# Emptying the bank of attention values: one ScalarE copy of all 128 partitions, a transfer between partitions, and GpSimd's add, in place of a ScalarE copy of 64 and VectorE's add

## The chip, the cores and the metric

The kernel runs on one core of a Trainium2 chip. A core has TensorE (PE; its weight loads are a row of their own, PEld), VectorE (DVE), ScalarE (ACT), GpSimd (POOL) and SyncE (SP), which issues the kernel's transfers. The metric is the device time of one execution, in microseconds. The kernel before took 1499.21 us, the median of three runs (1498.03 to 1502.22).

## What is computed

One layer of a streaming encoder, for one sequence of 1024 positions, 1024 channels, all in float32. Two attention branches of 8 heads of 64 channels run on one projection of the input; branch a is softmax attention over a band of the last 9 chunks of 64 positions with a learned bias by distance, branch b is stick-breaking attention:

```python
h = x @ w_in                                  # q, k, v of a; q, k, v of b; two gates
# a: softmax(q k^T / 8 + bias[distance]) @ v  over the own chunk and the 8 before it
# b: z = q k^T / 8;  w = sigmoid(z) * prod over keys between of (1 - sigmoid(z));  w @ v
y_a = chunk_band_attention(qa, ka, va, rel_bias) @ w_proj_a
y_b = stick_breaking_attention(qb, kb, vb) @ w_proj_b
mix = (sigmoid(ga + b_gate_a) * y_a + sigmoid(gb + b_gate_b) * y_b) @ w_out
x = layer_norm(alpha * x + mix, ln1_g, ln1_b)
g, u = split(x @ w_ffn_in)
x = layer_norm(alpha * x + (silu(g) * u) @ w_ffn_out, ln2_g, ln2_b)
```

## The kernel before

Matmul operands are float32 values split in two: `hi`, the value rounded to a shorter format that PE multiplies fast, and `lo`, the rest. `split` (L107) makes them: ScalarE copies `hi` (L108), VectorE subtracts for `lo` (L109). A product is then three matmuls, or two where one operand is kept as the pair.

The stages in time are: the input projection, 0 to about 355 us; the attention with what is laid between it, 355 to 687 us; branch b's output projection, the merge and the first norm; the feed-forward part, which ends the run. The change is in the attention.

There the work is in 8 pairs of heads (`i` 0 to 3 branch a, 4 to 7 branch b), two heads (`h` 0 and 1) to a pair and two groups of 512 queries (`g` 0 and 1) to a head. For each block of 128 queries a head makes a tile of attention weights (`soft_block`, L483, and `stick_block`, L513): scores on PE (L461, L462), then for a the sum with the bias and its minimum on VectorE (L492), the exponential on ScalarE (L497), the reciprocal on VectorE (L499) and the scaling on GpSimd (L500); for b two sigmoids on ScalarE (L525, L526), two running products on VectorE (L529, L533; their second input is a tile in PSUM) and the multiplication on GpSimd (L535). The value steps (`value_steps`, L537) then go through the key blocks, 8 of them for g = 0 and 4 for g = 1: `turn` transposes weights on PE (L556) into a PSUM bank `tp` and splits it to `pt`; `mult` multiplies with the values (L569, L570) into the bank `pv`.

The values of a head are kept as 128 columns, 64 of `hi` and 64 of `lo`, so that one matmul does both: the bank `pv` holds the products with `hi` in partitions 0 to 63 and those with `lo` in partitions 64 to 127. At the last key block of a group the bank is emptied: ScalarE copies the lower half to the head's 64 partitions of the pair's tile `yt` (L575), VectorE adds the upper half from PSUM (L576). There is one such bank (`BANKS`, `pv=1`). When all four quarters of a pair are in, SyncE stores the tile in `y_dr` (L578); for the pair i = 7 it stays in SBUF. `reload_y` (L624) brings the others back for the output projections.

Between the steps fill work is laid, for which a generator hands out single matmuls: the gate products (`gate`, L411; L418) and then branch a's output projection (L603; gated on VectorE, L606), 18 matmuls for each head of a and 42 for each of b (`FILL`). Weights for them, yraw and gA tiles are loaded by SyncE and split by ScalarE and GpSimd (L402, L630). The value step that is multiplied lags its transposes by two (`LAG`), and the weight blocks are made a given number ahead (`LEAD`).

The order on each engine isn't that of the source lines: a planner places the instructions engine by engine from the source order, the dependences and its own idea of costs, and every engine then runs its list in order. The tiles of a tag share the given number of buffers (`SLOTS`, here `yt=3`); one whose buffer is still read waits for it. All transfers are issued by SyncE, in its list's order; one that waits holds up those behind it.

Of the kernel before, what the change touches and what calls it, by code (L numbers as in the profile page):

```python
# [14 lines left out]
ALU = mybir.AluOpType  # L15
# [3 lines left out]
P = 128  # L19
# [3 lines left out]
DH = 64  # L23
# [23 lines left out]
def hybrid_trunk_kernel(ctx: ExitStack, tc, x, xt, w_in, b_gate, rel_bias, w_proj,  # L47
# [6 lines left out]
    nc = tc.nc  # L54
# [7 lines left out]
    def slot(tag, name, dtype=F32):  # L62
        return pool.tile([P, 1024], dtype, tag=tag, name=name, bufs=SLOTS[tag])
# [10 lines left out]
    def bank(tag, name):  # L74
        return ps.tile([P, HW], F32, tag=tag, name=name, bufs=BANKS[tag])

    def dram(name, n):
        return [dr.tile([P, 1024], F32, name=f"{name}{i}") for i in range(n)]
# [3 lines left out]
    dma = nc.sync.dma_start  # L82
# [12 lines left out]
    y_dr = dram("y_dr", 8)  # L95
# [11 lines left out]
    def split(dst_h, dst_l, src):  # L107
        nc.scalar.copy(dst_h, src)  # L108
        nc.vector.tensor_tensor(dst_l, src, dst_h.bitcast(F32), ALU.subtract)  # L109
# [325 lines left out]
    def load_qk(hd):  # L435

        i, h = hd["i"], hd["h"]
        n = 2 * i + h
        q, k = (d[i][h * P:(h + 1) * P] for d in (q_dr, k_dr))
        for key, part in (("qs", None), ("kh", 0), ("kl", DH)):  # L440
            t = hd[key] = slot(key, f"{key}{n}", F32R)
            if part is None:
                dma(t.bitcast(F32), q)
            else:
                for half in (slice(0, DH), slice(DH, P)):
                    dma(t[half].bitcast(F32), k[part:part + DH])
        if hd["br"] == 0:
            hd["bias"] = rel_bias_tile(hd["n"])

    def load_v(hd):  # L450

        n = 2 * hd["i"] + hd["h"]
        t = slot("v", f"v{n}", F32R)
        dma(t.bitcast(F32), v_dr[n])
        hd["v"] = t.rearrange("p (t c) -> p t c", t=8)
# [57 lines left out]
    def stick_block(hd, b, be):  # L513
# [7 lines left out]
        for c0, n in cuts:  # L521
# [12 lines left out]
                                             kp[:, s0 - 1:s0], ALU.mult, ALU.bypass)  # L534
            nc.gpsimd.tensor_tensor(be[:, m0:e], be[:, m0:e], kp[:, m0 - 1:e - 1], ALU.mult)  # L535

    def value_steps(hd, g, wt):  # L537

        br, h = hd["br"], hd["h"]
        reach = (4, 8)[br]  # L540
        q0 = 4 * g
        nm = f"{'ab'[br]}{hd['n']}_{g}"
        pv = []

        kbs = [4, 5, 6, 7, 3, 2, 1, 0] if g == 0 else [7, 6, 5, 4]
        steps = []
        for i, kb in enumerate(kbs):
            lo_q = max(q0, kb - reach)
            hi_q = min(q0 + 3, kb)
            n = (hi_q - lo_q + 1) * P  # L550
            pts = []

            def turn(kb=kb, lo_q=lo_q, hi_q=hi_q, n=n, pts=pts):
                tp = bank("tr", f"tp_{nm}_{kb}")
                for qb in range(lo_q, hi_q + 1):
                    tr(tp[:, (qb - lo_q) * P:(qb - lo_q + 1) * P],  # L556
                       wt[qb - q0][:, (kb - qb) * P:(kb - qb + 1) * P], ident)
                pt = slot("pt", f"pt_{nm}_{kb}", F32R)
                split(pt[:, 0:n], pt[:, HW:HW + n], tp[:, 0:n])
                pts.append(pt)  # L560

            def mult(i=i, kb=kb, lo_q=lo_q, n=n, pts=pts):
                v = hd["v"]
                if i == 0:
                    pv.append(bank("pv", f"pv_{nm}"))
                last = i == len(kbs) - 1
                cs = slice((lo_q - q0) * P, (lo_q - q0) * P + n)
                pt = pts[0]
                mm(pv[0][:, cs], v[:, kb, :], pt[:, 0:n], start=(i == 0), stop=False)  # L569
                mm(pv[0][:, cs], v[:, kb, :], pt[:, HW:HW + n], start=False, stop=last)  # L570
                if last:
                    yt = hd["yt"]()
                    r = slice(h * DH, (h + 1) * DH)
                    gs = slice(g * HW, (g + 1) * HW)
                    nc.scalar.copy(yt[r, gs], pv[0][DH:P])  # L575
                    nc.vector.tensor_tensor(yt[r, gs], pv[0][0:DH], yt[r, gs], ALU.add)  # L576
                    if h == 1 and g == 1 and hd["i"] < 7:
                        dma(y_dr[hd["i"]], yt)  # L578

            steps.append((turn, mult))  # L580
        return steps

# [57 lines left out]
    def fill_until(t):  # L640
        while state["t"] < t and not state["done"]:
            try:
                state["t"] += next(fill)
            except StopIteration:
                state["done"] = True
# [35 lines left out]
    for si, (hd, g, st, box) in enumerate(vsteps):  # L681
        hidx, pos = si // nhead, si % nhead
        if hidx < 15 and pos == 1:
            load_qk(heads[hidx + 1])
        if hidx < 15 and pos == 4:
            load_v(heads[hidx + 1])
        while wi < min(hidx * 8 + LEAD[pos], len(wunits)):
            wunits[wi]()
            wi += 1
        if st == 0:  # L690
            steps_of[(hidx, g)] = value_steps(hd, g, box)
        turn, mult = steps_of[(hidx, g)][st]
        turn()
        last = goal
        goal += FILL[hd["br"]] / nhead
        fill_until(0.5 * (last + goal))
        pend.append(mult)
        if len(pend) > LAG:
            pend.pop(0)()
        fill_until(goal)  # L700
# [361 lines left out]
```

## Time and profile before

| | us |
|---|---|
| median of three runs | 1499.21 |
| lowest, highest | 1498.03, 1502.22 |
| the profiled execution, its own time | 1501.38 |
| its span in the profile | 1499.3 |
| attention with its fill work | 355 to 687 |

In the page's rows and in answers on the trace, times are in us from the start of the span. A row of a group reads: line, engine, operation, output <- inputs, shapes, count | busy time, mean in ns | idle time of the engine just before it and who ended it. A row of a wait reads: who waited, on which line, <- for whom, total us, how often, the longest. A row of the timeline reads: start, length, instruction, and in brackets the idle time before it.

### The profile page before, as it was taken

To read this page: it belongs to the slowest core of one execution; us is meant where nothing else is said; L and a number is where in the kernel's file an instruction comes from. 1 tells how busy PE (TensorE), PEld (TensorE's weight loads), DVE (VectorE), ACT (ScalarE), POOL (GpSimd) and SP (SyncE) were. 2 spreads that over 40 slices of the span, in tenths; PEclk is the share of its full clock that TensorE was granted. 3 is DMA by queue.
4 is the path that set the end of the run, shared out by engine and by line. 5 is a ranking of instruction groups with operands and counts; after the bars stand their busy time and mean duration, and the time that the engine had idled before them with its cause. 6 is when DMAs were issued, how large, how long until landed. Compare 5 with 4: busy or idle time off the path is not lost. (4 is left out here: it accounts for less than half of the span.)

```text
span 1499.3 us, 19075 instructions
## 1 busy us (share of the span) xinstructions
PE 1440.3 (96%) x6728; PEld 1179.6 (79%) x6728; DVE 1043.9 (70%) x1702; ACT 679.7 (45%) x1174; POOL 282.4 (19%) x322
## 2 busy tenths in 40 slices
PE   8999999999999999899999899999999998999997
PEld 6788888887887777777787688888888886778886
DVE  8865556435878887887849966767777755767757
ACT  6444444336877778775303534444444433111201
POOL 0000000004344558650014000000000003341016
PEclk9999999999999999999999999999999999999999
DMA  6555555247754556647502123444444456677602
GB/s 211 163 175 169 168 168 170 98 144 213 206 170 142 159 165 204 187 157 280 183 0 87 62 100 121 152 155 155 155 155 154 155 189 232 245 249 267 234 8 105
DMA packets 81215, 244.05 MB, mean 163 GB/s; under 512 B 10064, under 2 KB 10064, under 8 KB 81120
## 3 DMA queue, kind: packets, MB, share of 16 engines
q1 hardware_dynamic: 81120, 242.84, 48.5%
q8 instruction: 53, 0.87, 0.2%
q14 instruction: 42, 0.34, 0.1%
HBM read 162.03 MB, written 80.77 MB: 162 GB/s over the span
## 5 line engine op out<-in xcount | busy, mean ns | idle before, releaser
L535 POOL TENSOR_TENSOR w_b<-w_b,kp_b 128x511 f32<-128x511 f32 (+3 forms) x96 | 97.5, 1021 | 51.5 <-DVE kp_b L533 40.6
L950 POOL TENSOR_TENSOR tda<-wdR,wdL 128x512 f32<-128x512 f32 x8 | 10.7, 1340 | 491.6 <-DMA wdR<-in_w_ffn_out_dram 477.8
L533 DVE TENSOR_TENSOR_SCAN kp_b<-kp_b,ident_ps 128x384 f32<-128x384 f32 (+6 forms) x88 | 78.3, 890 | 4.1
L479 POOL MEMSET bias<- 64x64 f32 x8 | 1.2, 146 | 334.5 <-ACT bias L478 334.5
L745 POOL TENSOR_TENSOR mv<-mv,neghalf 128x1 f32<-128x1 f32 x16 | 23.9, 1495 | 211.4 <-DVE mv L744 211.4
L525 ACT ACTIVATE kp_b<-sc_b 128x512 f32<-128x512 f32 (+3 forms) x96 | 48.5, 505 | 31.4 <-PE sc_b L462 26.5
L183 DVE TENSOR_TENSOR c<-sxp,c 128x512 f32<-128x512 f32 x16 | 11.1, 692 | 73.9 <-issue 40.7
L925 DVE TENSOR_TENSOR x<-dx,x 128x512 f32<-128x512 f32 x64 | 43.6, 689 | 24.6 <-PE dx L995 24.6
L109 DVE TENSOR_TENSOR pt_b<-tp_b,pt_b 128x512 fp32r<-128x512 f32 (+1 forms) x96 | 51.1, 543 | 10.9 <-ACT pt_b L108 10.4
L170 PE MATMUL szf<-x1S63h,wcf 128*128 128x512 f32 x176 | 57.8, 389 | 0.0
L500 POOL TENSOR_SCALAR w_a<-w_a,st_a 128x640 f32<-128x640 f32 (+2 forms) x64 | 42.6, 671 | 67.2 <-DVE st_a L499 49.6
L556 PE MATMUL tp_b<-ident,w_b 128*128 128x128 f32 x288 | 49.3, 277 | 5.2 <-DVE pt_b L109 2.8
L108 ACT CAST pt_b<-tp_b 128x512 fp32r<-128x512 f32 (+1 forms) x96 | 47.1, 497 | 13.7 <-PE tp_b L556 13.2
L109 DVE TENSOR_TENSOR sl<-h,sl 128x512 fp32r<-128x512 f32 x56 | 38.4, 686 | 20.2 <-ACT sl L108 20.2
L108 ACT CAST sl<-h 128x512 fp32r<-128x512 f32 x56 | 34.8, 621 | 35.6 <-PE syf L170 17.1
L109 DVE TENSOR_TENSOR pt_a<-tp_a,pt_a 128x512 fp32r<-128x512 f32 (+1 forms) x96 | 45.5, 484 | 7.6 <-ACT pt_a L108 7.3
L497 ACT ACTIVATE w_a<-w_a,st_a 128x640 f32<-128x640 f32 (+2 forms) x64 | 44.6, 698 | 12.8 <-DVE st_a L492 11.2
L118 PE MATMUL ops<-wh_o,ml 128*128 128x512 f32 x128 | 50.2, 392 | 0.2 <-DVE ml L109 0.2
L115 PE MATMUL ops<-wh_o,mh 128*128 128x512 f32 x128 | 50.2, 392 | 0.0
L116 PE MATMUL ops<-wl_o,mh 128*128 128x512 f32 x128 | 49.9, 390 | 0.0
L556 PE MATMUL tp_a<-ident,w_a 128*128 128x128 f32 x240 | 44.8, 277 | 5.0 <-POOL w_a L500 2.4
L833 ACT ACTIVATE h<-sxf 128x512 f32<-128x512 f32 x22 | 13.2, 598 | 79.6 <-PE sxf L170 79.6
(1881 smaller groups left out, 4833.4 us busy)
## 6 DMA issues: line engine op xcount, KB each, us to landing
s_dr<-sl SPq DMA_DIRECT2D x112, 256.0 KB, 2.2
sd<-s_dr SPq DMA_DIRECT2D x56, 512.0 KB, 5.2
wLf<-in_w_ffn_in_dram SPq DMA_DIRECT2D x22, 512.0 KB, 4.4
wRf<-in_w_ffn_in_dram SPq DMA_DIRECT2D x22, 512.0 KB, 3.6
wLp<-in_w_in_dram SPq DMA_DIRECT2D x17, 512.0 KB, 5.3
wRp<-in_w_in_dram SPq DMA_DIRECT2D x17, 512.0 KB, 4.0
v_dr<-v SPq DMA_DIRECT2D x16, 512.0 KB, 4.3
qs<-q_dr SPq DMA_DIRECT2D x16, 512.0 KB, 6.2
```

The source lines that it names most:

```text
L108: nc.scalar.copy(dst_h, src)
L109: nc.vector.tensor_tensor(dst_l, src, dst_h.bitcast(F32), ALU.subtract)
L115: mm(acc, lh, rh, start=(i == 0), stop=False)
L116: mm(acc, lh, rl, start=False, stop=False)
L118: mm(acc, ll, rh, start=False, stop=(i == n))
L170: mm(acc, lw[:, ks], rx, start=(first and kt == i == 0), stop=(kt == 3 and i == 2), skip_group_check=not first)
L497: nc.scalar.activation(s[:, 0:w], s[:, 0:w], AF.Exp, bias=st[:, m:m + 1], scale=-1.0, accum_out=st[:, 2:3])
L525: nc.scalar.activation(kp[:, c0:e], sc[:, 0:n], AF.Sigmoid, scale=-1.0)
L533: nc.vector.tensor_tensor_scan(kp[:, s0:e], kp[:, s0:e], ident_ps()[:, 0:e - s0], kp[:, s0 - 1:s0], ALU.mult, ALU.bypass)
L535: nc.gpsimd.tensor_tensor(be[:, m0:e], be[:, m0:e], kp[:, m0 - 1:e - 1], ALU.mult)
L556: tr(tp[:, (qb - lo_q) * P:(qb - lo_q + 1) * P], wt[qb - q0][:, (kb - qb) * P:(kb - qb + 1) * P], ident)
L925: nc.vector.tensor_tensor(dst, acc, dst, ALU.add)
```

## The change

For the pairs 0 to 6, ScalarE copies the whole bank, 128 partitions, in one instruction: to `yt` for the first head of the pair, to a new tile `yv` (one for each head, from the same three buffers) for the second. A transfer within SBUF then brings the half that lies on the wrong partitions to the head's own 64 partitions of the other tile. GpSimd adds the two. The add, and after the last one of a pair the store in `y_dr`, is put in a list and handed out three value steps later. VectorE's add of these 28 quarters is gone. The pair i = 7 is emptied as before.

```diff
+    later = []
+
     def value_steps(hd, g, wt):
...
                     yt = hd["yt"]()
                     r = slice(h * DH, (h + 1) * DH)
                     gs = slice(g * HW, (g + 1) * HW)
-                    nc.scalar.copy(yt[r, gs], pv[0][DH:P])
-                    nc.vector.tensor_tensor(yt[r, gs], pv[0][0:DH], yt[r, gs], ALU.add)
-                    if h == 1 and g == 1 and hd["i"] < 7:
-                        dma(y_dr[hd["i"]], yt)
+                    if hd["i"] == 7:
+                        nc.scalar.copy(yt[r, gs], pv[0][DH:P])
+                        nc.vector.tensor_tensor(yt[r, gs], pv[0][0:DH], yt[r, gs], ALU.add)
+                    else:
+
+                        if g == 0:
+                            hd["yv"] = slot("yt", f"yv_{nm}")
+                        yv = hd["yv"]
+                        both, other = (yt, yv) if h == 0 else (yv, yt)
+                        nc.scalar.copy(both[:, gs], pv[0])
+                        dma(other[r, gs], both[(DH, 0)[h]:(P, DH)[h], gs])
+
+                        def add():
+                            nc.gpsimd.tensor_tensor(yt[r, gs], yt[r, gs], yv[r, gs], ALU.add)
+                            if h == 1 and g == 1:
+                                dma(y_dr[hd["i"]], yt)
+                        later.append([3, add])
...
         turn, mult = steps_of[(hidx, g)][st]
+        for item in list(later):
+            item[0] -= 1
+            if item[0] == 0:
+                later.remove(item)
+                item[1]()
         turn()
```

## The prediction

> **What bounds the kernel now.** I read the page first, then the stretch in which the changed lines run, then who waits there, then single transitions.
>
> ```profile
> PE 1440.3 (96%) x6728; PEld 1179.6 (79%) x6728; DVE 1043.9 (70%) x1702; ACT 679.7 (45%) x1174; POOL 282.4 (19%) x322
> ...
> 355.00:493.00 138.00, 131.62 (x791) 110.29 (x790) 111.61 (x372) 110.67 (x275) 60.72 (x96) 1.00 0.59 173
> 493.00:655.00 162.00, 150.75 (x811) 121.46 (x810) 132.20 (x222) 122.09 (x266) 102.20 (x140) 1.00 0.58 182
> ```
>
> The page's first part gives TensorE (PE) 96% of the span. The two window rows (length, then busy time of PE, its weight loader PEld, VectorE, ScalarE, GpSimd, then clock) cut out the attention: 355 to 493 us is softmax attention (a), 493 to 655 stick-breaking (b) up to its last pair, i = 7, which the change leaves alone. PE is the fullest engine in both; the idle time that could be won is 138 - 131.6 = 6.4 us in a and 162 - 150.75 = 11.25 us in b. The granted clock is 1.00, so no term below is a clock effect. Who holds PE up (first the weight loader's waits in b, then PE's own in b, then the loader's in a):
>
> ```profile
> PEld pv_b L569 <- DVE yt L576: 12.1, 10, 2.1
> PEld tp_b L556 <- DVE pt_b L109: 4.7, 9, 1.1
> PEld tp_b L556 <- POOL w_b L535: 1.8, 2, 1.0
> ...
> PE pv_b L569 <- DVE yt L576: 8.1, 10, 1.6
> ...
> PEld sc_a L461 <- DVE st_a L492: 4.7, 14, 0.6
> PEld tp_a L556 <- POOL w_a L500: 4.0, 9, 0.7
> PEld tp_a L556 <- DVE pt_a L109: 3.5, 7, 1.1
> PEld pv_a L569 <- DVE yt L576: 1.0, 2, 0.6
> ```
>
> In b the wait that ends last is the one on line 576: the single pv bank is given back only when VectorE's add has read it. That is 8.1 us of PE's 11.25 us of idle time. In a it is 1.0 us. One such transition in b, in time (start, length):
>
> ```profile
> 580.81 0.28 PE L570 MATMUL pv_b<-pt_b,v 128*128 128x128 f32 x1
> ...
> 581.40 1.86 DVE L533 TENSOR_TENSOR_SCAN kp_b<-kp_b,ident_ps 128x192 f32<-128x192 f32 x2
> 581.47 0.58 ACT L575 COPY yt<-pv_b 64x512 f32<-64x512 f32 x1
> ...
> 583.75 0.68 DVE L576 TENSOR_TENSOR yt<-pv_b,yt 64x512 f32<-64x512 f32 x1
> ...
> 584.48 0.19 PEld L569 LDWEIGHTS pv_b<-pt_b,v 128*128 128x128 f32 x1 [1.81 <-DVE yt L576]
> ```
>
> ScalarE's copy ended at 582.05; the add stood behind two scans until 583.75, and the loader had been idle since 584.48 - 1.81 = 582.67. With the copy alone releasing the bank, the whole wait would be gone here, with 0.6 us to spare.
>
> **The change, part by part.** It touches 28 of 32 evacuations (i < 7): 16 in a, 12 in b.
>
> ```profile
> L421 ACT COPY gate<-gps 128x512 f32<-128x512 f32 x12 | 7.4, 614 | 0.0
> L575 ACT COPY yt<-pv_b 64x512 f32<-64x512 f32 x16 | 9.3, 584 | 1.0 <-PE pv_b L570 0.5
> L576 DVE TENSOR_TENSOR yt<-pv_b,yt 64x512 f32<-64x512 f32 x12 | 8.1, 679 | 0.4 <-ACT yt L575 0.2
> L535 POOL TENSOR_TENSOR w_b<-w_b,kp_b 128x512 f32<-128x512 f32 x13 | 16.7, 1288 | 2.4 <-DVE kp_b L533 1.8
> L535 POOL TENSOR_TENSOR w_b<-w_b,kp_b 128x511 f32<-128x511 f32 x13 | 16.7, 1287 | 11.4 <-DVE kp_b L533 10.0 <-ACT pt_b L108 1.3
> ```
>
> *ScalarE.* The copy goes from 64 to 128 partitions of the same 512 columns: between 584 ns (64 partitions) and 614 ns (another 128-partition copy from a bank). 28 x 0.03 = 0.8 us of ScalarE at most, and 0.03 us per release: nothing.
>
> *The wait in b.* Gone. Its worth lies between PE's idle time, 8.1 us, and the loader's, 12.1 us (a matmul's modelled end hides some of the gap): I take the middle, 10.1. I do not expect all of it on the clock. The next waits in the list, on pt_b and w_b (4.7 and 1.8 us), are met by VectorE and GpSimd while PE stands; when PE no longer stands, it asks earlier. VectorE at 132.2 of 162 us and ScalarE at 122.1 keep pace, but not without queues, so I give back a third: **-6.7 us**.
>
> *The wait in a.* Here the built program tells more than the diff. The order is planned anew, and between the last multiplication of one pv bank and the first of the next PE now holds fewer instructions. Where one head's last bank hands over to the next head, 17 became 7 (3 transposes, 2 gate products, 2 score products). The same place in the trace of before:
>
> ```profile
> 436.78 0.62 ACT L497 ACTIVATE w_a<-w_a,st_a 128x384 f32<-128x384 f32 x1 [0.50 <-DVE st_a L492]
> 436.92 0.31 PE L570 MATMUL pv_a<-pt_a,v 128*128 128x128 f32 x1
> 437.40 0.94 ACT L108 CAST pt_a<-tp_a 128x512 fp32r<-128x512 f32 x2
> 437.54 0.40 PE L418 MATMUL gps<-xl,wh_g 128*128 128x512 f32 x1
> 437.77 0.28 PE L461 MATMUL sc_a<-kh,qs 128*128 128x256 f32 x1
> 437.89 0.28 PE L462 MATMUL sc_a<-kl,qs 128*128 128x256 f32 x1
> 438.37 0.58 ACT L575 COPY yt<-pv_a 64x512 f32<-64x512 f32 x1
> ...
> L556 PEld LDWEIGHTS tp_a<-ident,w_a 128*128 128x128 f32 x231 | 29.0, 140 | 10.4 <-DVE pt_a L109 3.5 <-POOL w_a L500 3.4 <-POOL w_b L535 0.9
> ...
> 430.97 0.28 PE L570 MATMUL pv_a<-pt_a,v 128*128 128x128 f32 x1
> ...
> 431.44 0.58 ACT L575 COPY yt<-pv_a 64x512 f32<-64x512 f32 x1
> ```
>
> From start to start a gate product takes 437.77 - 437.54 = 0.23 us, a score product 0.12, a transpose 0.14: the 7 take 3 x 0.14 + 2 x 0.23 + 2 x 0.12 = 1.1 us. The copy, though, ended 438.95 - 436.92 = 2.0 us after the last product's start, because two casts of 0.94 us stood ahead of it on ScalarE. Behind the other kind of bank (second set of rows) it was 432.02 - 430.97 = 1.05 us. So PE waits between 0 and 0.9 us at each of 8 head changes. In the new order the casts' transposes come earlier but an exponential of that 0.62 us kind moves in between casts and copy: I take 0.4 us, nearer the low end since the casts start some half a microsecond sooner. 8 x 0.4 = **+3.2 us** (0 to 7.2); the old wait goes, **-0.7** (0.4 of PE, 1.0 of the loader). In b the new spacing is 1.6 us and 1.3 us by the same unit costs, against a copy that ends 582.05 - 580.81 = 1.24 us after: no wait, with little to spare at the head changes.
>
> *VectorE.* It loses 28 x 0.68 = 19 us, 10.9 of them in a, a tenth of its 111.6 us. PE's waits that come from VectorE in a (4.7 + 4.0 + 3.5 = 12.2 us; w_a hangs on its reciprocal) should ease by a tenth: **-1.2 us**.
>
> *The transfer.* 64 rows of 2 KB within SBUF, 28 times, on SyncE's queue. No such transfer is in the trace; the nearest are these (median us to landing last):
>
> ```profile
> s_dr<-sl SPq DMA_DIRECT2D x112, 256.0 KB, 2.2
> kl<-k_dr SPq DMA_DIRECT2D x32, 256.0 KB, 6.6
> y_dr<-yt SPq DMA_DIRECT2D x7, 512.0 KB, 4.2
> 442.19 0.83 POOL L500 TENSOR_SCALAR w_a<-w_a,st_a 128x256 f32<-128x256 f32 x2 [1.46 <-DVE st_a L499]
> ```
>
> Bounds 2.2 us (a store from SBUF) and 6.6 us (one of a burst of loads); I take 2.2, it also leaves SBUF and stands alone in the queue, and about 0.5 us of issue. The new order puts GpSimd's add behind instructions like the one at 442.19, which ends at 443.02, 4.1 us after that bank's copy ended at 438.95: landed at 2.7, the transfer is not waited for. At 6.6 the add would hold GpSimd for 3 us. The Trainium skill ("DMA: Bandwidth & Descriptors", the section on the anatomy of one DMA) has a fixed cost of about 2.0 us plus bytes at 436 GB/s; for 128 KB that would be an estimate of 2.3 us, and by it too GpSimd would not wait; it is stated for transfers issued by GpSimd, and no run shows it yet for this one.
>
> On SyncE the transfer waits for the copy, and the loads of q, k, v, gates and weights queue behind it; y_dr's store now waits for GpSimd, about 4.1 + 1.3 us after the copy. These loads fill slots freed one head ahead (138 us for 8 heads: 17 us in a, more in b), and in the list of waits PE never waits for a load in the attention: cost nothing; were that cover gone, 5 us at 7 stores, 35 us, would be the price. The extra tile per head takes its buffer from the three yt slots. The built program gives the one that y_dr's store frees last to a tile needed a head later: no wait.
>
> *GpSimd's add.* 512 columns of two SBUF inputs, by the row of that width 1.29 us; 28 of them are 36 us, 15.5 in b where GpSimd has 60 us idle. Behind it wait the w multiplies that PE's transposes need. PE waited on them 1.8 us in b, so there is slack; I take **+0.5 us**, bounds 0 and 15.5. The rows of 511 and 512 columns have the same mean (1287, 1288 ns) beside a busy VectorE. The Trainium skill ("SBUF — State Buffer", two separate sides) says that a GpSimd instruction reading SBUF and a VectorE one with two SBUF inputs lock each other out whole; VectorE's scans, splits and gate products here have one input in PSUM, so by that rule the adds stop none of them, which is why I give no chance to a slower VectorE.
>
> Sum: -6.7 + 3.2 - 0.7 - 1.2 + 0.5 = **-4.9 us**. The profiled execution took 1501.4 us (span 1499.3), 2.2 above the median of the three runs, 1499.2. It would become 1496.5; the median, 1494.3. A measurement of this kernel can tell about 0.3%, 4.5 us, from no change.
>
> **Rivals.** *The whole gain.* Nothing later is late, and ScalarE's copy is never late in a: -10.1 - 0.7 - 1.2 = -12, 1487. For it: PE is the fullest engine and 8.1 of 11.25 us hang on this wait. Against: the 1.1 us spacing in a.
>
> *ScalarE takes VectorE's place.* The wait on the bank changes its releaser: 8 x 0.9 = 7.2 us in a, and 12 waits of 0.2 in b where the spacing is as tight: -6.7 - 0.7 - 1.2 + 7.2 + 2.4 = +1, 1500. For it: the 2.0 us row; against: the earlier transposes.
>
> *GpSimd's queue makes it slower.* Each add stands in order before the next w multiply. If each of the 12 in b delays a transpose by its 1.29 us, or by landing time where the transfer lands late, PE loses 15.5 us instead of 0.5: -4.9 + 15 = +10, 1509; at two thirds of that, 1504. It outweighs the rest from (4.9 + 0.5)/12 = 0.45 us per add on. For it, GpSimd between 550 and 600 us:
>
> ```profile
> 550.00:600.00 50.00, 46.40 (x251) 37.23 (x250) 40.59 (x70) 42.66 (x89) 41.09 (x47) 1.00 0.63 199
> ```
>
> 41.1 of 50 us busy, and 4 adds fall there. Against: w blocks are made several steps ahead of their use, which is why PE waits for them so little.
>
> **How the numbers follow.** My forecast 0.45, own range 1490 to 1499 (bounds 8.1 and 12.1, 0 and 7.2): 0.27 of it faster by over 0.3%, 0.18 within. Whole gain 0.14, faster. ScalarE instead 0.14: 0.11 within, 0.03 slower. GpSimd's queue 0.27: 0.22 slower, 0.05 within. Faster 0.41, same 0.34, slower 0.25. The range takes in the whole gain and most of GpSimd's case: 1487 to 1506.
>
> **What would show it.** Right: in b the wait of pv on the evacuation falls from 12.1 us to under 2, PE's idle time there from 11.25 to about 5; in a pv waits on ScalarE's copy for about 3 us in 8 places; adds of 1.3 us whose idle time before them is not ended by the transfer. Wrong: the transfer lands later than 4 us after the copy and GpSimd stands on it; transposes wait for w_b by more than 6 us; or the waits on pt_b grow by as much as the wait on the bank shrinks.

## The result and the profile after

| | us |
|---|---|
| before, median of 8 runs beside the changed kernel | 1499.80 (1497.86 to 1502.22) |
| after, median of 8 runs | 1493.81 (1492.63 to 1498.39) |
| ratio, 95% interval | 0.9963 [0.9951, 0.9975] |
| after, the profiled execution, its own time | 1492.63 (span 1490.9) |

The change gains 6.0 us, 0.4%. The forecast was 1494.3. The two profiled executions lie further apart than the medians, 1501.38 - 1492.63 = 8.75 us: the one of before was 1.6 us above its median, the one of after 1.2 us below. So differences of single rows between the two traces carry 2.8 us that belong to the executions and not to the change.

The first line of the page of after, and the same two stretches of the windows view as in the prediction (length, then busy time of PE, PEld, VectorE, ScalarE, GpSimd, then clock):

```profile
PE 1436.5 (96%) x6728; PEld 1178.4 (79%) x6728; DVE 1026.0 (69%) x1674; ACT 674.2 (45%) x1174; POOL 318.1 (21%) x350
```

```profile
355.00:493.00 138.00, 131.00 (x791) 110.46 (x790) 103.64 (x355) 109.01 (x276) 79.35 (x111) 1.00 0.64 186
493.00:655.00 162.00, 154.71 (x839) 125.43 (x838) 130.14 (x219) 125.43 (x282) 123.76 (x156) 1.00 0.65 196
```

VectorE has 28 instructions fewer (1702 to 1674) and 17.9 us less, GpSimd 28 more and 35.7 us more. In b PE's idle time fell from 11.25 to 162 - 154.71 = 7.3 us, in a it went from 6.4 to 7.0. The second stretch of after takes in some of the last pair; from 491 to 646 us, about the work that before did from 493 to 655, PE's idle time is 155 - 148.56 = 6.4 us (the row stands with the experiments). The clock is 1.00 in both stretches, as before.

Where the time went is told best by one mark that both traces have: the start of the last multiplication into each pv bank, of which there are 32. Timeline rows of before (start, length, instruction) for the 1st, the 16th (end of a), the 17th and the 28th (the last in b that the change touches):

```profile
366.42 0.22 PE L570 MATMUL pv_a<-pt_a,v 128*128 128x128 f32 x1
...
490.07 0.31 PE L570 MATMUL pv_a<-pt_a,v 128*128 128x128 f32 x1
...
506.07 0.27 PE L570 MATMUL pv_b<-pt_b,v 128*128 128x128 f32 x1
...
641.67 0.28 PE L570 MATMUL pv_b<-pt_b,v 128*128 128x128 f32 x1
```

The same four of after (these lines stand two further down in its source):

```profile
366.15 0.22 PE L572 MATMUL pv_a<-pt_a,v 128*128 128x128 f32 x1
...
489.75 0.31 PE L572 MATMUL pv_a<-pt_a,v 128*128 128x128 f32 x1
...
505.24 0.27 PE L572 MATMUL pv_b<-pt_b,v 128*128 128x128 f32 x1
...
634.93 0.27 PE L572 MATMUL pv_b<-pt_b,v 128*128 128x128 f32 x1
```

Stretch a took 490.07 - 366.42 = 123.65 us before and 123.60 after: nothing. Stretch b took 641.67 - 506.07 = 135.60 us and then 634.93 - 505.24 = 129.69: 5.9 us less. Between the two stretches, from the 16th mark to the 17th, it was 16.00 us and then 15.49. These two stretches, "a" and "b" from here on, are what the experiments are read by.

The weight loader's waits in b of after (from 491 to 646 us), then PE's own there, then the loader's in a (353 to 491 us; who waited, for whom, total us, times, longest):

```profile
PEld tp_b L558 <- POOL w_b L535: 5.0, 6, 1.3
PEld tp_b L558 <- DVE pt_b L109: 4.7, 8, 1.1
PEld sc_b L461 <- ACT w_b L526: 1.9, 2, 1.6
...
PEld pv_b L571 <- ACT yt L586: 0.8, 2, 0.6
PEld pv_b L571 <- ACT yv_b L586: 0.6, 3, 0.3
```

```profile
PE tp_b L558 <- DVE pt_b L109: 4.0, 8, 1.0
PE sc_b L461 <- ACT w_b L526: 1.2, 1, 1.2
PE tp_b L558 <- POOL w_b L535: 0.5, 1, 0.5
PE pv_b L571 <- ACT yt L586: 0.2, 1, 0.2
```

```profile
PEld tp_a L558 <- POOL w_a L500: 5.4, 10, 0.9
PEld sc_a L461 <- DVE st_a L492: 4.7, 12, 1.1
PEld tp_a L558 <- DVE pt_a L109: 1.9, 2, 1.1
PEld pv_a L571 <- ACT yt L586: 1.4, 3, 0.5
PEld pv_a L571 <- ACT yv_a L586: 1.4, 3, 0.5
```

The wait on VectorE's add, 12.1 us of the loader and 8.1 of PE, is gone. What is left of the wait for the bank in b is 1.4 us on ScalarE's copy, 0.2 of it PE's. The loader's wait on w_b grew from 1.8 to 5.0 us, while PE's own fell from 1.4 to 0.5. PE's own wait on pt_b is now its largest in b; in the kernel before (493 to 655 us) it was

```profile
PE tp_b L556 <- DVE pt_b L109: 1.4, 4, 0.7
```

and the 1.2 us for the score products, which wait for a sigmoid on ScalarE, were not there at all. In a new waits of 2.8 us on ScalarE stand where 1.0 us on VectorE had been.

The transition that the prediction showed, in the timeline of after:

```profile
578.40 0.27 PE L572 MATMUL pv_b<-pt_b,v 128*128 128x128 f32 x1
...
578.59 1.86 DVE L533 TENSOR_TENSOR_SCAN kp_b<-kp_b,ident_ps 128x192 f32<-128x192 f32 x2
...
579.25 0.64 ACT L586 COPY yv_b<-pv_b 128x512 f32<-128x512 f32 x1
...
579.92 0.48 SPq L587 DMA_DIRECT2D yt<-yv_b  x1
...
579.95 0.19 PEld L571 LDWEIGHTS pv_b<-pt_b,v 128*128 128x128 f32 x1
```

The same two scans hold VectorE until 580.45, but the bank's release no longer stands behind them: the copy ended at 579.89 and the loader, with no idle time before it, goes on at 579.95. From the last product of one bank to the first weights of the next it was 584.48 - 580.81 = 3.7 us and is now 1.55.

### The profile page after: what moved, and what is told of

The parts are those of the page before. It is cut to its first block, busy times and chain, and to the rows that moved or that the text cites. A ratio compares the mean times of both kernels' runs of the same rounds, so it can differ in the third digit from the quotient of the medians.

```text
span 1490.9 us, 19151 instructions
## 1 busy us (share of the span) xinstructions
PE 1436.5 (96%) x6728; PEld 1178.4 (79%) x6728; DVE 1026.0 (69%) x1674; ACT 674.2 (45%) x1174; POOL 318.1 (21%) x350
## 4 chain that ended last, share of the span: by engine, by line
PE 74%; DVE 10%; DMA 4%; POOL 4%; ACT 3%; issue 3%; SPq 0%; POOLq 0%; DVEq 0%; ACTq 0%
PE sxf L170 15%; PE sxp L170 11%; PE szf L170 8%; PE szp L170 6%; PE dx L1015 5%; PE syf L170 4%; PE syp L170 3%; PE dz L1015 2%; DVE kp_b L533 2%; PE gps L418 2%; PE ops L118 2%; PE ops L116 2%; PE ops L115 2%; PE tp_a L558 1%; PE fpswh_h L115 1%
## 5 line engine op out<-in xcount | busy, mean ns | idle before, releaser
L558 PEld LDWEIGHTS tp_b<-ident,w_b 128*128 128x128 f32 x288 | 34.0, 140 | 20.7 <-DVE pt_b L109 7.1
L526 ACT ACTIVATE w_b<-sc_b 128x511 f32<-128x511 f32 (+3 forms) x96 | 49.4, 515 | 0.0
```

The source lines that it names most:

```text
L526: nc.scalar.activation(be[:, m0:e], sc[:, m0 - c0:n], AF.Sigmoid)
L558: tr(tp[:, (qb - lo_q) * P:(qb - lo_q + 1) * P], wt[qb - q0][:, (kb - qb) * P:(kb - qb + 1) * P], ident)
```

## The experiments

The theory: all of the gain is that the bank is released in b by ScalarE's copy instead of VectorE's add. Rivals: VectorE's relief (28 adds fewer) does it; part of it comes from a; the GpSimd add, or the transfer before it, costs a large part again. A rival that no run separates is the order: every kernel here is planned anew, and a part of each difference can come from that. Each ratio below stands against the kernel before, run beside it on the same chip: 1499.80 us beside the changed kernel, 1500.46 beside the next four, 1499.85 beside the four after them, 1500.14 beside the last two. The ratios are not quite the quotients of these medians (for b alone that would be 0.9954), and medians of different groups are compared by what each gained.

| kernel | median, us | ratio | a, us | b, us |
|---|---|---|---|---|
| before | 1499.80 | 1 | 123.65 | 135.60 |
| after | 1493.81 | 0.9963 [0.9951, 0.9975] | 123.60 | 129.69 |
| change in b alone | 1493.53 | 0.9945 [0.9929, 0.9962] | 123.61 | 130.39 |
| change in a alone | 1500.10 | 0.9996 [0.9985, 1.0007] | 123.56 | 135.87 |
| add on VectorE | 1499.98 | 1.0 [0.9988, 1.0012] | 128.88 | 131.41 |
| no add | 1490.39 | 0.9928 [0.9912, 0.9945] | 123.51 | 127.90 |
| two copies, no transfer | 1505.08 | 1.0037 [1.0019, 1.0054] | 129.99 | 133.29 |
| add one step later, not three | 1492.55 | 0.995 [0.9938, 0.9963] | 123.56 | 129.90 |
| also half of the last pair | 1495.02 | 0.996 [0.9946, 0.9974] | 123.56 | 130.20 |
| VectorE given 12 instructions in b | 1494.61 | 0.9963 [0.9949, 0.9976] | 123.58 | 133.16 |
| b alone, add one step later | 1492.93 | 0.9953 [0.9941, 0.9965] | 123.62 | 129.68 |
| after, once more | 1491.77 | 0.9948 [0.9934, 0.9962] | 123.53 | 130.27 |

The columns a and b are from one trace each, by the marks above. The two traces of after differ by 0.6 us in b; less than about that is not read from them there. In a ten of the twelve traces lie within 0.15 us of each other.

**In b alone.**

```diff
-                    if hd["i"] == 7:
+                    if hd["i"] == 7 or hd["br"] == 0:
                         nc.scalar.copy(yt[r, gs], pv[0][DH:P])
                         nc.vector.tensor_tensor(yt[r, gs], pv[0][0:DH], yt[r, gs], ALU.add)
+                        if h == 1 and g == 1 and hd["i"] < 7:
+                            dma(y_dr[hd["i"]], yt)
```

> The change in stick-breaking attention alone (pairs 4 to 6); softmax attention is emptied as before. Theory 1, the bank's earlier release is what gains: 6.4 us of the traces' gain lay in b, so about -5 to -6.5 us against the kernel before (ratio 0.996), PE's wait of pv_b on VectorE's evacuation near 0. Rival, VectorE's relief is what gains: b holds 8.1 of its 19 us, so under half of the gain, -2.5 us.

All of the gain is there: 1493.53 beside a before of 1500.46.

**In a alone.** The same with the condition `hd["br"] == 1`, so that b and the last pair are emptied in the old way.

> The change in softmax attention alone (pairs 0 to 3). Theory 1: a had 1 us of waits on the bank and kept 2.8 us of new ones on ScalarE's copy, so 0 to -1 us against before. Rival, VectorE's relief: 10.9 of its 19 us are in a, so -3.5 us.

Nothing: the interval takes in 1, and in the stretches a is level while b is as before, 135.87 us, a second trace for the 135.60. Its loader's wait in b is to the digit the one of before:

```profile
PEld pv_b L571 <- DVE yt L579: 12.1, 10, 2.0
```

The two runs together say that the gain is in b, and that the 16 copies, transfers and adds in a bring and cost nothing that the medians can tell. What they do bring is at the handover: from the 16th mark to the 17th it is 15.5 us in the changed kernel (both traces), in this run and in four others that change a, and 16.0 in the three that leave a as it was.

**The add on VectorE.** Copy and transfer stay; VectorE adds the two tiles from SBUF, three steps later. The bank is released as in the changed kernel, but VectorE gets its instruction back.

```diff
-                            nc.gpsimd.tensor_tensor(yt[r, gs], yt[r, gs], yv[r, gs], ALU.add)
+                            nc.vector.tensor_tensor(yt[r, gs], yt[r, gs], yv[r, gs], ALU.add)
```

> The changed kernel, but VectorE makes the later adds, from SBUF; the bank is still given back by ScalarE's copy. Theory 1: the gain stays, -5 to -7 us against before, and the waits on w_b by GpSimd go back from 5.0 towards 1.8 us. Rival, VectorE's relief: the gain goes, 0 to -1 us.

This missed: no gain at all. The stretches show two things. In b 4.2 of the 5.9 us stay, so the release is worth most of what it was; in a 5.2 us are lost that neither kernel lost before. The adds themselves (duration in ns: least, median, most):

```profile
L590 DVE TENSOR_TENSOR yt<-yt,yv_a x16: 665/689/1752, 371.7 to 501.7; 64x512 f32<-64x512 f32 x16
L590 DVE TENSOR_TENSOR yt<-yt,yv_b x12: 674/1212/2791, 516.6 to 649.0; 64x512 f32<-64x512 f32 x12
```

The old add, one input in PSUM, took 679 ns. In b most of the new ones are longer; in a 13 of 16 are not, so their length is not where the time in a went. What the trace shows in a is VectorE standing on the transfer ahead of the add, three times, 2.2 us in all, and PE standing on VectorE behind that:

```profile
395.40 0.69 DVE L590 TENSOR_TENSOR yt<-yt,yv_a 64x512 f32<-64x512 f32 x1 [1.12 <-DMA yt<-yv_a]
...
397.14 0.42 PE L461 MATMUL sc_a<-kh,qs 128*128 128x320 f32 x1 [1.36 <-DVE st_a L492]
```

Between the 4th and the 5th mark, where this lies, the run loses 1.4 us against the changed kernel, and 1.2 us between the 12th and the 13th around another such wait (463.08, 0.77 us). The rest of the 5.2 us is not traced.

In b another thing comes in. The longest of the adds in the timeline, beside what GpSimd did at that time:

```profile
574.54 2.79 DVE L590 TENSOR_TENSOR yt<-yt,yv_b 64x512 f32<-64x512 f32 x1 [1.56 <-DMA yv_b<-yt]
```

```profile
572.02 4.77 POOL L645 TENSOR_TENSOR yl<-yraw,yh 128x1024 fp32r<-128x1024 f32 x2
576.74 1.18 POOL L535 TENSOR_TENSOR w_b<-w_b,kp_b 128x255 f32<-128x255 f32 x1
```

GpSimd's two subtractions end at 576.79. The add began in the middle of them and ended at 577.33, 0.54 us after them: it has the length of a wait for GpSimd's instruction and then its own work. The other way round, a w_b multiplication of 511 columns took 1.78 us instead of 1.29 where an add had begun just ahead of it:

```profile
616.93 0.67 DVE L590 TENSOR_TENSOR yt<-yt,yv_b 64x512 f32<-64x512 f32 x1
...
616.98 1.78 POOL L535 TENSOR_TENSOR w_b<-w_b,kp_b 128x511 f32<-128x511 f32 x1 [0.48 <-DVE kp_b L533]
```

This is what the Trainium skill ("SBUF — State Buffer", two separate sides) says of a VectorE instruction with two SBUF inputs and a GpSimd instruction that reads SBUF: whichever starts first holds the shared port for the whole instruction. The trace agrees in these two places. So the experiment changed three things at once, the engine, the port and the list in which the transfer is waited for. Its total says nothing on VectorE's relief, and how the loss divides between the port and the wait for the transfer stays open. In its waits VectorE's work for PE is late everywhere: the loader waited 10.6 us on pt_b in b (after: 4.7) and 7.1 us on st_a in a (4.7).

**VectorE as busy as before, without that port.** To the changed kernel 12 VectorE instructions are added in b, at the place of the old add, one input in PSUM, 8.2 us in all; none took longer than 0.70 us, beside a GpSimd that is busy for 116 of 155 us. They change no value that is read: for a pair's second head they write the values that are there already, for its first head a half of `yv` that nobody reads.

```diff
                         dma(other[r, gs], both[(DH, 0)[h]:(P, DH)[h], gs])
+                        if hd["br"] == 1:
+                            q = slice((DH, 0)[h], (P, DH)[h])
+                            nc.vector.scalar_tensor_tensor((yv, yt)[h][q, gs], ident_ps()[q], 0.0,
+                                                           yt[q, gs], ALU.mult, ALU.add)
```

> The changed kernel, and in b VectorE is given back as much work as it lost: 12 instructions of 64x512 with one input in PSUM, that change no value and hold no bank. Theory 1, the release of the bank: -4 to -6 us against before still, 0 to +2 against the changed kernel. Rival, VectorE's relief: the 8 us of work return and with them most of the gain, +4 to +6 against the changed kernel.

It stays at 1494.61, 0.9963, the ratio of the changed kernel. The windows view from 491 to 646 us, of this kernel, then of after, then of before:

```profile
491.00:646.00 155.00, 146.65 (x794) 117.94 (x791) 127.24 (x215) 116.04 (x259) 116.15 (x149) 1.00 0.64 189
```

```profile
491.00:646.00 155.00, 148.56 (x809) 120.95 (x807) 122.95 (x207) 118.68 (x265) 118.02 (x153) 1.00 0.66 195
```

```profile
491.00:646.00 155.00, 143.64 (x773) 115.60 (x774) 127.50 (x214) 117.99 (x257) 100.14 (x132) 1.00 0.57 177
```

VectorE is as busy as in the kernel before, 127.2 against 127.5 us, and by the medians 5.2 us of gain are still there. So the gain does not need VectorE's relief. How much the relief adds stays open: 0.8 or 3.1 us by the medians (against the first and the second run of the changed kernel), 3.5 us in stretch b of the trace, which is of the slowest of its runs, 1496.76.

**No add.**

```diff
                         def add():
-                            nc.gpsimd.tensor_tensor(yt[r, gs], yt[r, gs], yv[r, gs], ALU.add)
+                            pass
```

> The changed kernel without GpSimd's 28 adds (the parts from hi and lo are not summed; copy and transfer stay). Theory 1 with a price for GpSimd's queue: the 3.2 us by which waits on w_b grew come back at most, so 0 to -3 us against the changed kernel, -6 to -9 against before. If the adds cost nothing on the path: the same as the changed kernel.

This kernel leaves out the sum of the two halves, so it is a measure and not a version to use. It gains 10.1 us against the kernel before, where the changed kernel gained 6.0 and, once more, 8.4: by the medians the adds cost 4.1 or 1.7 us, each uncertain by 2 to 3 us. By the stretches they cost 129.69 - 127.90 = 1.8 us in b (2.4 against the second trace of after), 0.15 us for each of 12, and 0.1 in a. The loader's wait on w_b, which one would lay to them, is there without them:

```profile
PEld tp_b L558 <- POOL w_b L535: 4.8, 5, 1.3
```

So it does not come from GpSimd's longer list; that PE asks earlier would explain it, which no run shows by itself. Where the adds do cost is one place. From the 22nd mark to the 23rd the changed kernel takes 578.40 - 560.17 = 18.2 us, without the adds 16.7: 1.5 of the 1.8 us. In the changed kernel the add of 557.77 stands on GpSimd ahead of the subtraction (L645) that frees the buffer of a weight load. SyncE issues the load at its end, and ScalarE then waits for the landing; first the changed kernel, then the one without adds:

```profile
561.44 0.81 SPq L400 DMA_DIRECT2D wr_y<-in_w_proj_dram  x2
...
565.77 1.05 ACT L401 CAST wh_y<-wr_y 128x1024 fp32r<-128x1024 f32 x1 [1.04 <-DMA wr_y<-in_w_proj_dram]
```

```profile
559.94 0.81 SPq L400 DMA_DIRECT2D wr_y<-in_w_proj_dram  x2
```

Without the adds the same cast begins at 564.36 with no such wait before it. The sigmoids behind it on ScalarE are late by about as much, and PE's one wait of 1.2 us on a sigmoid, at 571.62, is gone too. The second trace of after has both waits, 1.2 us on ScalarE and 1.3 on PE.

**Two copies.** ScalarE copies each half by itself onto the head's partitions of two tiles; there is no transfer, and GpSimd adds as before.

```diff
-                        both, other = (yt, yv) if h == 0 else (yv, yt)
-                        nc.scalar.copy(both[:, gs], pv[0])
-                        dma(other[r, gs], both[(DH, 0)[h]:(P, DH)[h], gs])
+                        nc.scalar.copy(yt[r, gs], pv[0][DH:P])
+                        nc.scalar.copy(yv[r, gs], pv[0][0:DH])
```

> No transfer: ScalarE empties the bank with two copies of 64 partitions, hi and lo rows each straight to the head's partitions, and GpSimd adds. The bank is given back some 0.6 us later and ScalarE does 16 us more. Theory 1: the wait on the bank, 12 us in b before, comes back only where the second copy is late, 0.2 to 0.5 us 12 times; -2 to -5 us against before, 1 to 4 above the changed kernel. If the transfers cost the changed kernel something (its queue, GpSimd's waits), this one comes out level with it or faster.

Slower than before, 1505.08; this missed as well. A copy of 64 partitions costs 0.58 us like one of 128, so the bank is held 0.58 us longer, and the loader now waits for the second copy in nearly every place (first in a, 355 to 500 us; then in b, 491 to 646):

```profile
PEld pv_a L571 <- ACT yv_a L586: 6.9, 13, 0.9
```

```profile
PEld pv_b L571 <- ACT yv_b L586: 6.0, 11, 0.9
```

By the stretches a is 6.4 us longer than in the changed kernel. In b it takes 133.29 us, 3.6 more than the changed kernel and still 2.3 less than before. The waits on the copy, 12.9 us of the loader where the changed kernel has 4.2, are only a part: PE's own are 3.8 us in a and 1.1 in b, and in b PE now waits 2.9 us for GpSimd to clear a column of w_b (L518), a wait that PE's list in the changed kernel does not have. ScalarE also has 28 instructions more (1174 to 1202). So the transfer, which leaves ScalarE with one copy, is what makes the change pay; how the loss divides between the later release, ScalarE's longer list and the order on PE, planned anew here too, stays open.

**The add handed out one step later instead of three.**

```diff
-                        later.append([3, add])
+                        later.append([1, add])
```

> The adds are handed out one value step after the copy, not three. A step is 1.4 us in a and 2.1 in b, so each add stands at GpSimd 2.7 to 4.1 us sooner, ahead of a transfer that lands 2.5 to 2.8 us after its issue. Rival of the prediction (GpSimd's queue): GpSimd then stands on the transfer and PE on w, +4 to +10 us against the changed kernel. If the slack of the weight blocks covers it: within 1.5 us of the changed kernel.

Level with the changed kernel. GpSimd then waited 3.1 us in 5 places for transfers, all of them in a (2.5 us in 4 in the changed kernel), and it cost nothing.

**Half of the last pair too.** The condition `hd["i"] == 7` becomes `hd["i"] == 7 and h == 1`, so that 30 of 32 quarters are emptied in the new way.

> The new way for the first head of the last pair too (30 quarters of 32). Theory 1: PE's waits on the bank there were 0.2 us twice and 1.5 us at the end of the first head; -0.5 to -1.5 us against the changed kernel. VectorE's relief alone would give -0.3.

No further gain, where 0.5 to 1.5 us were expected: 1495.02. By the trace the last pair, from the 28th mark to the 32nd, took 45.20 us against 42.29 in the changed kernel. Of its waits one on the old add is left, 2.2 us at once, on the head that is still emptied in the old way; PE waits 1.8 us there, and 2.5 on pt_b (1.2 in the changed kernel). Why the last pair is longer is not shown.

**In b alone, handed out one step later,** as a version that might beat both, run beside the changed kernel once more.

> The change in branch b alone (a is emptied as before), and the add handed out one value step later instead of three. If the gain is the release of the bank in b and nothing else counts, as the runs so far say, this is level with the changed kernel: 5 to 7 us below the kernel before, ratio 0.9955 to 0.9965, and within 1.5 us of the changed kernel run beside it. If the 16 copies, transfers and adds in a cost something after all that only their earlier VectorE relief hides, it is 2 us or more below the changed kernel. If the earlier adds in b hold up the w multiplications that the later ones let pass, it is 2 us or more above it.

> The changed kernel itself, timed beside the version that changes b alone: 1493 to 1495 us, ratio 0.9955 to 0.997 as in its first runs.

1492.93 and 1491.77, with intervals that overlap almost wholly. The version does as much with 12 transfers and adds instead of 28, but it is not faster. The changed kernel itself came out a little below what was expected of it. No version here that makes the sums beats it by what can be measured.

## Why the prediction was right, step by step

- **The wait in b.** Said to go, worth 6.7 us. It went from 12.1 us to 1.4 of the loader, from 8.1 to 0.2 of PE. The prediction gave back a third of 10.1, 3.4 us, to the next waits. That step held: PE's wait on pt_b grew from 1.4 to 4.0 us and one of 1.2 us on a sigmoid came, while the one on w_b fell from 1.4 to 0.5, 2.9 us in all. Without the adds b is 135.60 - 127.90 = 7.7 us shorter, so this term was 1 us too small (what VectorE's relief adds in b is in the 7.7).
- **GpSimd's add.** Said to cost 0.5 us, by the w multiplies that stand behind it. It is 1.8 by the stretch b, 1.7 to 4.1 by the medians: the term was mis-sized, too small by 1 us or more, though 0.15 us per add (at most 0.34 by the medians) is still below the 0.45 from which on the change would have been slower. Its way was another too: 1.5 of the 1.8 us come through one load, whose buffer is freed by an instruction that the add holds up. The prediction set loads at nothing because PE never waits for one; ScalarE did, and PE for ScalarE. The two errors in b cancel: -6.7 + 0.5 = -6.2 forecast, -5.9 measured.
- **The new wait in a.** Said to be 3.2 us in 8 places; it is 2.8 us in 6. One of them, at the place that the prediction showed, in the timeline of after:

```profile
436.81 0.28 PE L572 MATMUL pv_a<-pt_a,v 128*128 128x128 f32 x1
...
437.15 0.62 ACT L497 ACTIVATE w_a<-w_a,st_a 128x384 f32<-128x384 f32 x1
...
437.76 0.57 ACT L586 COPY yt<-pv_a 128x512 f32<-128x512 f32 x1
...
438.39 0.50 PE L571 MATMUL pv_a<-pt_a,v 128*128 128x512 f32 x1 [0.25 <-ACT yt L586]
```

  The exponential does stand ahead of the copy, and PE waits 0.25 us, the loader 0.46. PE itself loses less than its loader; its group in a has 1.5 us in all:

```profile
L571 PE MATMUL pv_a<-pt_a,v 128*128 128x512 f32 x24 | 10.2, 427 | 1.5 <-ACT yt L586 0.8 <-ACT yv_a L586 0.7
```

- **The rest of a.** The sum for a was +3.2 - 0.7 - 1.2 = +1.3; measured is -0.05, and the run with the change in a alone says the same. Gone are the old wait of 1.0 and 1.6 us on pt_a (3.5 to 1.9), about as much as the new wait brought. The sum had a loss of 1.3 us here that isn't there: PE's own part of the new wait is half of the 3.2.
- **The copy of 128 partitions.** 584 ns in a, 635 and 642 in b, against 584 for 64: nothing, as said.
- **The transfer.** 2.2 us taken, 2.5 to 2.8 measured (size, then median us from issue to landing), and the add is hardly ever held by it:

```profile
yv_a<-yt SPq DMA_DIRECT2D x8, 128.0 KB, 2.8
yt<-yv_a SPq DMA_DIRECT2D x8, 128.0 KB, 2.5
```

```profile
L590 POOL TENSOR_TENSOR yt<-yt,yv_b x12: 1282/1292/1302, 510.5 to 640.4; 64x512 f32<-64x512 f32 x12
...
  DMA yt<-yv_a: 1.9, 3
...
  DMA yv_a<-yt: 0.6, 1
```

  In b no add waited. The estimate of 2.3 us from the Trainium skill ("DMA: Bandwidth & Descriptors", anatomy of one DMA) was 0.2 to 0.5 us short, for a transfer that SyncE issued. The adds take 1.28 to 1.30 us, as the row of the w multiplication had it.
- **The last pair.** Said to be untouched. It is 1.2 us shorter in the trace (43.51 to 42.29), and 1.0 to 1.6 us shorter in every other version that leaves it alone, also in the one with the change in a alone. The version with the change in a alone works in b and in the last pair as before does, and has 1.0 of the 1.2 us. So most of it is not the change's; the one trace of before, of an execution 1.6 us above its median, may be long here, which is not shown.
- **The sum.** Forecast -4.9; the marks give -5.9 in b, -0.05 in a and -0.5 between them, the medians -6.0, and -8.4 when it was run once more (1500.14 to 1491.77). The path was right: the wait on the bank in b, gone by ScalarE's copy, carries the gain. That the number came so near is in part luck, since in b the gain of the release and the price of the adds were each too small by about as much; the 1.1 us that are left are the loss in a that did not come.
- **The rivals.** The whole gain (1487) did not come: the adds cost something and PE meets pt_b next, as said. ScalarE does take VectorE's place in a, but for 2.8 us that other waits give back. The queue of GpSimd costs by the trace a third of what would decide.
- **What would show it.** The wait in b under 2 us: yes. PE's idle time in b about 5: it is 7.3, or 6.4 over the same work. Some 3 us on ScalarE in a: yes. Transposes waiting for w_b by more than 6 us: 5.0 of the loader, close to the bound, and not because of the adds. Waits on pt_b growing by as much as the wait on the bank shrinks: PE's grew by 2.6 us where that one shrank by 7.9.

## What to carry to other kernels

In this kernel a bank with a single buffer cost what its release was late, and it was best given back by the engine that could do it in one instruction, with the rest of the work done later from SBUF by another. That engine's list is to be read for what else hangs on it: of twelve adds one, ahead of the instruction that frees a load's buffer, made 1.5 of their 1.8 us. With two copies in place of one the change no longer paid. When work leaves a PSUM operand for two SBUF operands, see what shares the SBUF port and in whose list the transfer is waited for: twelve instructions of the add's size in VectorE's list, one input in PSUM, cost between 0.8 and 3.5 us in b, and the 28 adds from SBUF the whole gain.

## What the runs showed of the hardware

- A VectorE add of two SBUF inputs, 64x512, took 0.67 us at the least and up to 2.79 us where GpSimd's instructions on SBUF had begun before it; the median was 0.69 in a and 1.21 in b. A GpSimd multiplication of 511 columns went from 1.29 to 1.78 us behind one.
- ScalarE's copy out of PSUM, 512 columns, costs the same for 64 partitions (0.58 us) as for 128 (0.58 to 0.64), and GpSimd's add of 64x512 the same (1.29) as its multiplication of 128x512.
- A transfer of 128 KB within SBUF, 64 rows of 2 KB from one half of the partitions to the other, lands 2.5 to 2.8 us after its issue, and occupies the issuing queue for 0.48 us.
